# Substitution products in a buffer of their own, low weight parts on VectorE, gate weights a tile ahead: a change to a two-layer hybrid encoder on one core

## The chip, the core and the metric

The kernel runs on one core of a Trainium2 chip. The metric is the device time of one execution in microseconds (us). All data is float32; products that need full precision are made from operands split in a high part (a rounded copy, type fp32r) and a low part (the rest), so that one product costs three matmuls.

The engines are named as the profile names them: PE (matmuls; PEld is its weight load), DVE (VectorE), ACT (ScalarE), POOL (GpSimd) and SP, which here only issues DMAs.

## What is computed

Two layers of an encoder over 1040 positions (16 meta tokens and 1024 inputs) and 1024 channels. Cut to what matters here:

```python
def hybrid_mixer(h, ...):
    proj = h @ w_in                       # q, k, v, z, gates b and a, short-conv channels
    qkv = silu(depthwise_conv(qkv)); q, k = l2norm(q), l2norm(k)
    beta = sigmoid(b_raw); g = -exp(a_log) * softplus(a_raw + dt_bias)
    o = chunk_gated_delta_rule(q, k, v, g[0], beta[0]) \
        + flip(chunk_gated_delta_rule(flip(q), flip(k), flip(v), flip(g[1]), flip(beta[1])))
    o = rms_normalised(o) * dn_norm_w * silu(z)
    y_sc = sc_b * depthwise_conv(sc_c * sc_h)
    return concat(o, y_sc) @ w_out

h = h + hybrid_mixer(rmsnorm(h)); h = h + swiglu(rmsnorm(h))     # twice, then a last rmsnorm
```

The delta rule works in chunks and for each chunk and head it solves a unit triangular system A = I + M, with M = strict triangle of (beta k) k^T times a decay. The kernel uses chunks of 128 and inverts A: forward substitution in the 32 x 32 blocks of the diagonal, and matmuls that join the blocks.

## The kernel before, in words

The activations lie transposed (channels on the partitions, 1040 positions along the row). A dense product (`dense`) takes one tile of 128 output channels in three chunks of 346 to 348 positions, each in a PSUM bank of its own: eight times three matmuls, and then an evacuation on DVE. Three banks carry the name `acc`. The weights of a tile come in two halves of 128 x 512: a DMA into `raw`, the high part on ACT (`wsplit`, L127), the low part on POOL (L128). `lov[0]` would send the low part to DVE; before, it is False throughout.

Order: the program is planned ahead. Each instruction has a priority, which is its place in the program unless it is set otherwise; a planner simulates the run with estimated durations, and each engine then works off its instructions in the fixed order that comes out. `at_prio` sets the running priority. `evp[0]` is a rank far ahead of all others (the layer's base less 60000), used for the evacuations of `dense`; with None they have their place in the program. `mmp[0]` puts dense matmuls of the later tiles behind other PE work. `after(ins, prev)` adds an order between two instructions. A tile with a tag shares a buffer with others of the same tag, and its first writer waits for the last user of the one before.

In each layer:

- Input tiles 4 to 7 (k), then 0 to 3 (q), positions `pos` 0 to 7 of a loop: dense product, evacuation (multiplied by the norm's `rstd`, L283; in the first one or two tiles a copy, L288, because `rstd` is late), convolution (L295 on ACT, L296 and L297 on DVE), silu and square on ACT, sums of squares on PE, `normalise` (L402). The weights of the next tile are loaded at the end of each turn.
- After `pos` 2, `gates()`: weights of 16 gate columns (L316 DMA, L317 high part, L318 low part, in a slot of the `raw` and `whi` rings), a product (L325), small operations. `gt`, in the buffer P0, is its working space.
- At `pos` 4 to 6, `chunk_p`: k k^T of each chunk (L439), the decay with the mask `off` (L443), their product (L448) into P0 and P1, the systems of the two directions.
- `sub_start` copies the diagonal blocks (L501) and transposes them (L503); `substitute(d)`, for directions 0 and 1, runs 31 steps of two DVE operations each: a product of a column of W and a row of Xi (L513), and its subtraction from Xi (L514). All 32 blocks lie along the rows of 128 partitions, so that each works on 128 x (j+1)(31-j) elements. Before, the product is put, transposed, into a part of W that is no longer read; L514 reads it transposed again. The two directions have nothing in common and are interleaved by the planner.
- `invert(d)` transposes the result (L523, L524) and joins the blocks with small matmuls (L543, L549, L555, L567) and copies on ACT.
- Beside these, tiles 8 to 11 (v), each with `v_store` (transposes on PE; L641 copies the first 16 positions, `vm`, on DVE), then z and short-convolution tiles; `chunk_a` makes the attention parts; then the scan over chunks, the output projection and the feed-forward part.

In the program, `substitute(0)` stands ahead of the v tiles, `invert(0)` behind the first of them, `substitute(1)` behind the second and `invert(1)` behind the third.

Of the kernel before, what the change touches and what calls it, by code (L numbers as in the profile page):

```python
# [7 lines left out]
F32 = mybir.dt.float32  # L8
F32R = mybir.dt.float32r
BF16 = mybir.dt.bfloat16  # L10
AF = mybir.ActivationFunctionType
ALU = mybir.AluOpType
# [10 lines left out]
WK = 4  # L23
# [3 lines left out]
C_ID, C_UT, C_LT, C_NF, C_NB, C_SEL, C_SEL2, C_MISC = 0, 128, 256, 384, 512, 640, 656, 672  # L27
# [13 lines left out]
def trunk(ctx: ExitStack, tc: tile.TileContext, xT, w_in, w_ba, w_out, w_gu, w_dn,  # L41
          par_d, alog_d, dtb_d, cst_d, eye_d, out):
    nc = tc.nc
    sb = ctx.enter_context(tc.tile_pool(name="sb", bufs=1))
    wp = ctx.enter_context(tc.tile_pool(name="wp", bufs=3))
# [4 lines left out]
    def nm(p):  # L50
        cnt[0] += 1
        return f"{p}_{cnt[0]}"

    def big(tag, dt=F32):
        return sb.tile([128, 4, L], dt, tag=tag, name=nm(tag))

    def row(tag, dt=F32, bufs=1):
        return sb.tile([128, L], dt, tag=tag, bufs=bufs, name=nm(tag))

    def t2k(tag):  # L60
        return sb.tile([128, 4, 128], F32, tag="ck2", bufs=5, name=nm(tag))

    def c4k(tag="c"):
        return sb.tile([128, L], F32, tag="c", bufs=2, name=nm(tag))
# [4 lines left out]
    def pa():  # L69
        return bank("a")  # L70
# [16 lines left out]
    def after(ins, prev):  # L87

        if prev is not None:
            tc.add_manual_dep(ins.ins, prev.ins.name, dep, reason="order")  # L90
        return ins

    def at_prio(p):
        tc.cur_priority = p
# [3 lines left out]
    tt = nc.vector.tensor_tensor  # L98
# [3 lines left out]
    dma = nc.sync.dma_start  # L102
# [14 lines left out]
    evp = [None]  # L117
    jobs = []
    lov = [False]
# [133 lines left out]
    epsq = sb.tile([128, 1], F32, name="epsq")  # L253
    nc.vector.memset(epsq, HD * EPS)
    cols["eps"] = epsc
    off = sb.tile([128, 2, 128], F32, name="off")
    dma(off.rearrange("p a b -> p (a b)"), cst_d[:, C_NF:C_NF + 256])
    alog = sb.tile([128, 2, 8], F32, name="alog")
    dtb = sb.tile([128, 2, 8], F32, name="dtb")
    dma(alog, alog_d.partition_broadcast(128))  # L260
# [4 lines left out]
    for l in range(DEPTH):  # L265
# [2 lines left out]
        pcol = lambda c: par[:, l * P_L + c:l * P_L + c + 1]  # L268
        rstd = ss
        base = tc.cur_priority  # L270
        evp[0] = base - 60000


        o0 = 16 if last else 0
        ochunks = TAIL if last else FULL
# [1 line left out]
        def inproj(i, evac, pool=None, chunks=FULL):  # L277
            ws = pre.pop(i) if i in pre else wload(w_in[l, i], KT)
            dense(ws, x, chunks, evac, pool)

        def to_row(t):
            def f(ps, n0, n1):
                tt(out=t[:, n0:n1], in0=ps, in1=rstd[:, n0:n1], op=ALU.mult)  # L283
            return f

        def to_row_late(t):
            def f(ps, n0, n1):
                nc.vector.tensor_copy(t[:, n0:n1], ps)  # L288
            return f

        def trow():
            return row(Y[1], F32, 3)

        def conv(src, dst, wc):
            act(out=dst, in_=src, func=AF.Copy, scale=pcol(wc + 1))  # L295
            stt(out=dst[:, 1:L], in0=src[:, 0:L - 1], scalar=pcol(wc), in1=dst[:, 1:L], op0=ALU.mult, op1=ALU.add)  # L296
            stt(out=dst[:, 0:L - 1], in0=src[:, 1:L], scalar=pcol(wc + 2), in1=dst[:, 0:L - 1], op0=ALU.mult, op1=ALU.add)  # L297
# [11 lines left out]
        m0d = dram.tile([2, 2, 4, 16, 16], F32, name=nm("m0d"))  # L309
        rsd = [dram.tile([4, 260], F32, name=nm("rsd")) for _ in range(2)]  # L310


        def gates():
            wr = wp.tile([128, WK, 128], F32, tag="raw", bufs=2, name=nm("war"))[:, 0, :].rearrange("p (k m) -> p k m", k=8)
            wb = wp.tile([128, WK, 128], F32R, tag="whi", name=nm("wba"))[:, 0:2, :].rearrange("p a (b m) -> p (a b) m", m=32)
            dma(wr, w_ba[l])  # L316
            act(out=wb[:, :, 0:16], in_=wr, func=AF.Copy)  # L317
            tt(out=wb[:, :, 16:32], in0=wr, in1=wb[:, :, 0:16].bitcast(F32), op=ALU.subtract)  # L318
            gt = big("P0")
            bat = gt[:, 0, :]  # L320
            for (n0, n1) in FULL:
                ps = pacc()
# [19 lines left out]
            for d in range(2):  # L342
                tt(out=sv[0][:, 36 * d:36 * d + 36].rearrange("p (c h) -> p c h", c=9), in0=psv[:, :, 1, 4 * d:4 * d + 4],
                   in1=dtb[:, l, 4 * d:4 * d + 4].unsqueeze(1).to_broadcast([128, 9, 4]), op=ALU.add)
# [18 lines left out]
            for d in range(2):  # L363
                tt(out=g[:, d], in0=sv[0][:, 36 * d:36 * d + 36].rearrange("p (c h) -> p c h", c=9),
                   in1=nA[:, 4 * d:4 * d + 4].unsqueeze(1).to_broadcast([128, 9, 4]), op=ALU.mult)
# [51 lines left out]
        P0 = [sb.tile([16, 4, 16], F32, tag=f"P0{d}", name=nm("P0")) for d in range(2)]  # L417
# [70 lines left out]

        tmp0 = []
        subs = {}  # L490

        def sub_start():

            tmp0.append(big(Y[0][2]))
            v = [tmp0[0][:, i, 0:1024] for i in range(4)]
            for d in range(2):
                W, Xi = (v[0], v[2]) if d == 0 else [c4k("x")[:, 0:1024] for _ in range(2)]
                W, Xi, dg = (t.rearrange("p (a b) -> p a b", a=32) for t in (W, Xi, v[3 - 2 * d]))
                dma(Xi, eye_d)
                for b in range(4):  # L500
                    act(out=dg[B[b]], in_=Pv[d][B[b], :, B[b]], func=AF.Copy)  # L501

                nc.vector.transpose(out=W, in_=dg.rearrange("p q i -> p i q"))  # L503
                subs[d] = W, Xi

        def substitute(d):
            W, Xi = subs[d]
            for j in (range(0, 31) if d == 0 else range(31, 0, -1)):
                i0, i1, a0, a1 = (j + 1, 32, 0, j + 1) if d == 0 else (0, j, j, 32)
                sh = [128, a1 - a0, i1 - i0]  # L510

                Tm = W[:, a0:a1, i0:i1]
                tt(out=Tm, in0=W[:, i0:i1, j:j + 1].rearrange("p i o -> p o i").to_broadcast(sh), in1=Xi[:, j:j + 1, a0:a1].rearrange("p o a -> p a o").to_broadcast(sh), op=ALU.mult)  # L513
                tt(out=Xi[:, i0:i1, a0:a1], in0=Xi[:, i0:i1, a0:a1], in1=Tm.rearrange("p a i -> p i a"), op=ALU.subtract)  # L514

        def invert(d):
            P_ = Pv[d]
# [70 lines left out]
        seq = (4, 5, 6, 7, 0, 1, 2, 3)  # L588
        for pos, i in enumerate(seq):
            hh = pos % 4  # L590
            t = trow()
            late = pos < (2, 1)[l]
            inproj(i, to_row_late(t) if late else to_row(t), pfirst if l == 0 and pos == 1 else None)
            if late:
                tt(out=t, in0=t, in1=rstd, op=ALU.mult)
            dst = (QT if i < 4 else KTt)[:, hh, :]
            conv(t, dst, P_CV + 3 * i)
            act(out=dst, in_=dst, func=AF.Silu)
            act(out=t, in_=dst, func=AF.Square)
            jobs.append(lambda w="qk"[i >= 4], q=hh, t=t: sums(w, q, t))  # L600
            if pos == 2:
                g, negG, nGb, negE, gl, bkd = gates()
            nxt = seq[pos + 1] if pos < 7 else 8
            if nxt not in pre:
                pre[nxt] = wload(w_in[l, nxt], KT)
            if pos == 4:
                jobs.extend([lambda c=c: k_out(c) for c in range(9)])
            if pos in (4, 5, 6):
                for c in range(3 * pos - 12, 3 * pos - 9):
                    chunk_p(c)  # L610
        sub_start()
        substitute(0)


# [12 lines left out]
        def low(f):  # L627

            here = tc.cur_priority
            at_prio(mmp[0])  # L630
            f()
            mmp[0] = tc.cur_priority
            at_prio(here)

        def v_store(i, v, c0):

            ps = pa()
            if c0 == 0:
                low(lambda: nc.tensor.transpose(ps[0:16, 0:128], v[:, 0:16], ident))
                vm = t2k("vm")[0:16, 0, :]  # L640
                nc.vector.tensor_copy(vm, ps[0:16, 0:128])  # L641
                dma(vkd[0, 0:16, 0, i * 128:(i + 1) * 128], vm)
            else:
                vt = v[:, 16 + 128 * (c0 - 1):16 + 128 * (c0 + 3)]
                for c in range(4):
                    low(lambda: nc.tensor.transpose(ps[:, c * 128:(c + 1) * 128], vt[:, 128 * c:128 * c + 128], ident))
                act(out=vt, in_=ps, func=AF.Copy)
                adma(vkd[c0:c0 + 4, :, 0, i * 128:(i + 1) * 128].rearrange("c p e -> p c e"), vt.rearrange("p (c e) -> p c e", c=4))

        ca = [0, 1, 8, 2, 7, 3, 6, 4, 5]  # L650
        for i in range(4):
            t = trow()
            inproj(8 + i, to_row(t))
            v = trow() if i % 2 == 0 else row(Y[1] + "f")
            conv(t, v, P_CV + 3 * (8 + i))
            act(out=v, in_=v, func=AF.Silu)
            jobs.extend([lambda i=i, v=v, c0=c0: v_store(i, v, c0) for c0 in (0, 1, 5)])
            if i == 0:
                invert(0)
            elif i == 1:  # L660
                substitute(1)
            elif i == 2:
                invert(1)
            if i > 0:
                for c in ca[3 * i - 3:3 * i]:
                    chunk_a(c)
# [164 lines left out]
        for i in range(4):  # L831
            t = trow() if i < 2 else hb[1][:, i, :] if i < 3 else y3
# [95 lines left out]
        for m in range(KT + 2):  # L928
# [4 lines left out]
            k = m - 2  # L933
# [106 lines left out]
        for f in range(FT):  # L1040
# [6 lines left out]
            W = {}  # L1047
# [8 lines left out]
            end = f == FT - 1  # L1056
# [105 lines left out]
        for gi, grp in enumerate(GROUPS):  # L1162
# [19 lines left out]
            if gi == 0:  # L1182

                w2 = {}
                for m in range(0, KT, 2):
                    hi, lo = (wp.tile([128, WK, 128], F32R, tag=t, name=nm(t)) for t in ("whi", "wlo"))
                    raw = raw4(("raw", "ck2")[m // 2 % 2])
# [104 lines left out]
```

## Time and profile before

| | us |
|---|---|
| median of 3 runs (2689.06 to 2693.82) | 2690.77 |
| the profiled execution, its own time | 2690.32 |
| its span, first to last instruction | 2688.5 |
| granted clock over the span | 0.98 |

Times in the profile count from the start of the span. A page gives the busy time of each engine; views of it give the same for stretches of time, list who waited for whom (in total, how often, the longest), or list single instructions: start, duration, engine, line, operation, output and inputs, shapes, and in brackets the idle time of the engine before it with what ended it. The clock is the share of full speed at which PE was allowed to run.

### The profile page before, as it was taken

The page shows a single profiled execution, that of the slowest core. Times are in us where ns is not written, and L with a number is a line of the kernel's source. Part 1 is how long each engine was busy: PE and PEld are TensorE (multiplying, and loading weights), DVE is VectorE, ACT ScalarE, POOL GpSimd, SP SyncE. Part 2 cuts the span into 40 slices and gives each one's busy share as a digit, 9 for nine tenths or more (in the row PEclk, how much of TensorE's full clock was granted, in tenths as well). Part 3 has the DMA queues.
Part 4 walks back from the last instruction along what each step waited for, and adds up shares of the span by engine and source line. Part 5 has one row for each costly group of instructions (what it writes and reads, how often), then busy time and mean ns, then how long its engine had stood idle before and what let it go on. Part 6 is the DMA issues. An engine that isn't in the chain of part 4 may idle for free. (4 is left out here: it accounts for less than half of the span.)

```text
span 2688.5 us, 43950 instructions
## 1 busy us (share of the span) xinstructions
PE 2564.2 (95%) x17274; PEld 2348.5 (87%) x17274; DVE 1533.5 (57%) x2245; ACT 985.8 (37%) x1785; POOL 1129.2 (42%) x823
## 2 busy tenths in 40 slices
PE   7988999999999999999999889999999999999997
PEld 6988889988999999999998878899877888887886
DVE  6787333548766566622355874345587766644226
ACT  4663322435333333321245633134452333332224
POOL 3353121225666666543222322212267766663341
PEclk9999899999999999999999989999999999999998
DMA  3532585434312222532224425766342222225321
GB/s 106 153 123 87 167 263 184 158 119 142 108 60 72 86 77 76 189 112 69 75 89 144 139 79 170 254 197 211 98 132 94 63 82 75 91 88 182 93 81 63
DMA packets 181492, 326.13 MB, mean 121 GB/s; under 512 B 21681, under 2 KB 58805, under 8 KB 181285
## 3 DMA queue, kind: packets, MB, share of 16 engines
q1 hardware_dynamic: 147972, 272.64, 31.0%
q10 hardware_dynamic: 30496, 42.09, 5.2%
q0 software_dynamic: 2816, 8.59, 1.0%
q8 instruction: 136, 2.23, 0.3%
q14 instruction: 72, 0.58, 0.1%
HBM read 239.66 MB, written 83.58 MB: 120 GB/s over the span
## 5 line engine op out<-in xcount | busy, mean ns | idle before, releaser
L128 POOL TENSOR_TENSOR wlo<-raw,whi 128x512 fp32r<-128x512 f32 (+2 forms) x264 | 337.7, 1282 | 1015.4 <-ACT whi L127 852.7
L154 PE MATMUL pacc<-a,whi 128*128 128x346 f32 (+2 forms) x1031 | 349.5, 342 | 13.3 <-ACT whi L127 6.4
L156 PE MATMUL pacc<-a,wlo 128*128 128x346 f32 (+2 forms) x1031 | 347.7, 340 | 4.1 <-POOL wlo L128 4.1
L127 ACT ACTIVATE whi<-raw 128x512 fp32r<-128x512 f32 (+2 forms) x264 | 151.3, 577 | 509.6 <-PE pacc L155 286.7
L154 PE MATMUL pacc<-b,whi 128*128 128x346 f32 (+2 forms) x882 | 307.1, 349 | 9.9 <-DVE a L283 9.4
L155 PE MATMUL pacc<-a,whi 128*128 128x346 f32 (+2 forms) x916 | 312.4, 342 | 2.7 <-DVE a L838 2.6
L156 PE MATMUL pacc<-b,wlo 128*128 128x346 f32 (+2 forms) x882 | 305.6, 349 | 0.3 <-POOL wlo L128 0.3
L155 PE MATMUL pacc<-b,whi 128*128 128x346 f32 (+2 forms) x776 | 267.8, 346 | 0.0
L154 PEld LDWEIGHTS pacc<-a,whi 128*128 128x128 f32 x1031 | 198.7, 193 | 25.5 <-ACT whi L127 7.4
L156 PEld LDWEIGHTS pacc<-a,wlo 128*128 128x128 f32 x1031 | 198.6, 193 | 11.6 <-POOL wlo L128 4.7
L154 PEld LDWEIGHTS pacc<-b,whi 128*128 128x128 f32 x882 | 168.8, 192 | 23.8 <-DVE a L283 10.8
L155 PEld LDWEIGHTS pacc<-a,whi 128*128 128x128 f32 x916 | 176.8, 193 | 10.2 <-DVE a L838 2.8
L156 PEld LDWEIGHTS pacc<-b,wlo 128*128 128x128 f32 x882 | 168.9, 192 | 11.4 <-issue 1.0
L981 POOL TENSOR_TENSOR wlo<-rw,whi 128x512 fp32r<-128x512 f32 x92 | 134.8, 1467 | 72.5 <-ACT whi L980 66.9
L155 PEld LDWEIGHTS pacc<-b,whi 128*128 128x128 f32 x776 | 148.6, 192 | 8.5 <-issue 0.4
L981 POOL TENSOR_TENSOR a<-rw,a 128x512 fp32r<-128x512 f32 x64 | 107.0, 1675 | 66.9 <-ACT a L980 66.9
L981 POOL TENSOR_TENSOR b<-rw,b 128x512 fp32r<-128x512 f32 x64 | 90.2, 1412 | 85.1 <-ACT b L980 53.4
L843 DVE TENSOR_TENSOR a<-pacc,a 128x346 f32<-128x346 f32 (+2 forms) x116 | 57.8, 500 | 109.4 <-PE pacc L156 109.2
L980 ACT ACTIVATE whi<-rw 128x512 fp32r<-128x512 f32 x92 | 57.8, 631 | 140.3 <-DVE rw L1054 72.8
L843 DVE TENSOR_TENSOR b<-pacc,b 128x512 f32<-128x512 f32 (+1 forms) x88 | 52.5, 599 | 98.9 <-PE pacc L156 98.1
L1055 DVE TENSOR_TENSOR rw<-raw,rw 128x512 f32<-128x512 f32 x44 | 97.2, 2208 | 1.2
L1050 DVE TENSOR_TENSOR rw<-rw,rw 128x512 f32<-128x512 f32 x44 | 66.9, 1521 | 48.1 <-POOL wlo L981 31.4
(813 smaller groups left out, 7365.7 us busy)
## 6 DMA issues: line engine op xcount, KB each, us to landing
raw<-in_w_in SPq DMA_DIRECT2D x112, 256.0 KB, 2.6
raw<-in_w_gu SPq DMA_DIRECT2D x104, 256.0 KB, 2.9
rw<-in_w_gu SPq DMA_DIRECT2D x88, 256.0 KB, 2.8
rec<-aqd SPq DMA_DIRECT2D x62, 256.0 KB, 4.1
rec<-vkd SPq DMA_DIRECT2D x61, 256.0 KB, 3.7
raw<-in_w_dn SPq DMA_DIRECT2D x60, 256.0 KB, 2.8
raw<-in_w_out SPq DMA_DIRECT2D x48, 256.0 KB, 3.0
a<-ad SPq DMA_DIRECT2D x20, 520.0 KB, 3.9
```

The source lines that it names most:

```text
L127: act(out=hi, in_=raw[:, 0:kk, :], func=AF.Copy)
L128: (tt if lov[0] else ptt)(out=lo, in0=raw[:, 0:kk, :], in1=hi.bitcast(F32), op=ALU.subtract)
L154: mm(ps[:, :n], wh, xh[:, n0:n1], start=(k == 0), stop=False)
L155: mm(ps[:, :n], wh, xl[:, n0:n1], start=False, stop=False)
L156: mm(ps[:, :n], wl, xh[:, n0:n1], start=False, stop=(k == K - 1))
L843: tt(out=hr[m][:, n0:n1], in0=ps, in1=hr[m][:, n0:n1], op=ALU.add)
L980: act(out=hi, in_=src, func=AF.Copy)
L981: ptt(out=lo, in0=src, in1=hi.bitcast(F32), op=ALU.subtract)
L1050: tt(out=s1t, in0=A21, in1=A22, op=ALU.add)
L1055: tt(out=A21, in0=A11, in1=A21, op=ALU.subtract)
```

## The change

- The mask `off` is loaded in each layer, into a buffer of 1 KB a partition with the tag `off`. When the layer is done with it, that buffer becomes `Tm`, for the products of the substitution.
- The product is laid out as rows of Xi are (i, then a), densely packed in `Tm`. Its operands are a column of W, broadcast along the inner dimension, and a row of Xi, broadcast along the outer one; the subtraction reads three operands with an inner step of one element.
- Direction 1's first product is ordered behind direction 0's last subtraction.
- `lov[0]` is True from `pos` 4 until `substitute(1)` has been put down, so the low parts of tiles 1, 2, 3, 8 and 9 of each layer go to DVE.
- The gate weights are loaded and split at the start of `pos` 2, ahead of that tile's product, into free parts of P0 and P1.
- The evacuations get their rank from `pos` 2 on, not from the start of the layer.
- The copy L641 gets the rank of the evacuations.

```diff
--- before.py
+++ after.py
@@ -253,8 +253,6 @@
     epsq = sb.tile([128, 1], F32, name="epsq")
     nc.vector.memset(epsq, HD * EPS)
     cols["eps"] = epsc
-    off = sb.tile([128, 2, 128], F32, name="off")
-    dma(off.rearrange("p a b -> p (a b)"), cst_d[:, C_NF:C_NF + 256])
     alog = sb.tile([128, 2, 8], F32, name="alog")
     dtb = sb.tile([128, 2, 8], F32, name="dtb")
     dma(alog, alog_d.partition_broadcast(128))
@@ -268,8 +266,6 @@
         pcol = lambda c: par[:, l * P_L + c:l * P_L + c + 1]
         rstd = ss
         base = tc.cur_priority
-        evp[0] = base - 60000
-
 
         o0 = 16 if last else 0
         ochunks = TAIL if last else FULL
@@ -309,14 +305,20 @@
         m0d = dram.tile([2, 2, 4, 16, 16], F32, name=nm("m0d"))
         rsd = [dram.tile([4, 260], F32, name=nm("rsd")) for _ in range(2)]
 
-
-        def gates():
-            wr = wp.tile([128, WK, 128], F32, tag="raw", bufs=2, name=nm("war"))[:, 0, :].rearrange("p (k m) -> p k m", k=8)
-            wb = wp.tile([128, WK, 128], F32R, tag="whi", name=nm("wba"))[:, 0:2, :].rearrange("p a (b m) -> p (a b) m", m=32)
+        off = sb.tile([128, 2, 128], F32, tag="off", name=nm("off"))
+        dma(off.rearrange("p a b -> p (a b)"), cst_d[:, C_NF:C_NF + 256])
+
+
+        gt = big("P0")
+        wr = gt[:, 3, 0:128].rearrange("p (k m) -> p k m", k=8)
+        wb = big("P1", F32R)[:, 0, 0:256].rearrange("p (k m) -> p k m", k=8)
+
+        def gate_weights():
             dma(wr, w_ba[l])
             act(out=wb[:, :, 0:16], in_=wr, func=AF.Copy)
             tt(out=wb[:, :, 16:32], in0=wr, in1=wb[:, :, 0:16].bitcast(F32), op=ALU.subtract)
-            gt = big("P0")
+
+        def gates():
             bat = gt[:, 0, :]
             for (n0, n1) in FULL:
                 ps = pacc()
@@ -488,10 +490,13 @@
 
         tmp0 = []
         subs = {}
+        Tm = None
 
         def sub_start():
 
+            nonlocal Tm
             tmp0.append(big(Y[0][2]))
+            Tm = sb.tile([128, 2, 128], F32, tag="off", name=nm("Tm")).rearrange("p a b -> p (a b)")
             v = [tmp0[0][:, i, 0:1024] for i in range(4)]
             for d in range(2):
                 W, Xi = (v[0], v[2]) if d == 0 else [c4k("x")[:, 0:1024] for _ in range(2)]
@@ -505,13 +510,14 @@
 
         def substitute(d):
             W, Xi = subs[d]
+            prev = subs.get("end")
             for j in (range(0, 31) if d == 0 else range(31, 0, -1)):
                 i0, i1, a0, a1 = (j + 1, 32, 0, j + 1) if d == 0 else (0, j, j, 32)
-                sh = [128, a1 - a0, i1 - i0]
-
-                Tm = W[:, a0:a1, i0:i1]
-                tt(out=Tm, in0=W[:, i0:i1, j:j + 1].rearrange("p i o -> p o i").to_broadcast(sh), in1=Xi[:, j:j + 1, a0:a1].rearrange("p o a -> p a o").to_broadcast(sh), op=ALU.mult)
-                tt(out=Xi[:, i0:i1, a0:a1], in0=Xi[:, i0:i1, a0:a1], in1=Tm.rearrange("p a i -> p i a"), op=ALU.subtract)
+                sh = [128, i1 - i0, a1 - a0]
+                t = Tm[:, 0:sh[1] * sh[2]].rearrange("p (a b) -> p a b", a=sh[1])
+                after(tt(out=t, in0=W[:, i0:i1, j:j + 1].to_broadcast(sh), in1=Xi[:, j:j + 1, a0:a1].to_broadcast(sh), op=ALU.mult), prev)
+                prev = None
+                subs["end"] = tt(out=Xi[:, i0:i1, a0:a1], in0=Xi[:, i0:i1, a0:a1], in1=t, op=ALU.subtract)
 
         def invert(d):
             P_ = Pv[d]
@@ -588,6 +594,10 @@
         seq = (4, 5, 6, 7, 0, 1, 2, 3)
         for pos, i in enumerate(seq):
             hh = pos % 4
+            if pos == 2:
+                gate_weights()
+                evp[0] = base - 60000
+            lov[0] = pos > 3
             t = trow()
             late = pos < (2, 1)[l]
             inproj(i, to_row_late(t) if late else to_row(t), pfirst if l == 0 and pos == 1 else None)
@@ -638,7 +648,11 @@
             if c0 == 0:
                 low(lambda: nc.tensor.transpose(ps[0:16, 0:128], v[:, 0:16], ident))
                 vm = t2k("vm")[0:16, 0, :]
+                here = tc.cur_priority
+                at_prio(evp[0])
                 nc.vector.tensor_copy(vm, ps[0:16, 0:128])
+                evp[0] = tc.cur_priority
+                at_prio(here)
                 dma(vkd[0, 0:16, 0, i * 128:(i + 1) * 128], vm)
             else:
                 vt = v[:, 16 + 128 * (c0 - 1):16 + 128 * (c0 + 3)]
@@ -659,6 +673,7 @@
                 invert(0)
             elif i == 1:
                 substitute(1)
+                lov[0] = False
             elif i == 2:
                 invert(1)
             if i > 0:
```

## Prediction

> **What bounds the kernel now.** I read the head of the page first, then the busy time by stage, then who waits for whom on PE, then single instructions in order of time.
>
> ```profile
> span 2688.5 us, 43950 instructions
> ...
> PE 2564.2 (95%) x17274; PEld 2348.5 (87%) x17274; DVE 1533.5 (57%) x2245; ACT 985.8 (37%) x1785; POOL 1129.2 (42%) x823
> ```
>
> PE is busy for 2564 of 2688 us, so a change that leaves its matmuls alone, as this one does, can only win part of the other 124 us, and what a throttled clock costs. The busy time by stage (columns PE, PEld, DVE, ACT, POOL, then the granted clock) shows where the diff's stages stand in this:
>
> ```profile
> 100.00:160.00 60.00, 55.71 (x371) 52.02 (x370) 42.31 (x55) 45.13 (x94) 32.95 (x71) 0.97 0.71 223
> 160.00:245.00 85.00, 69.67 (x448) 65.94 (x447) 82.30 (x158) 34.08 (x41) 27.84 (x15) 0.90 0.21 67
> ...
> 1440.00:1500.00 60.00, 55.56 (x382) 51.65 (x375) 43.54 (x56) 44.98 (x97) 28.63 (x46) 1.00 0.70 227
> 1500.00:1590.00 90.00, 73.18 (x448) 64.91 (x447) 85.34 (x158) 37.09 (x44) 21.80 (x15) 0.92 0.24 73
> ```
>
> 160 to 245 and 1500 to 1590 are the substitution stages of the two layers. DVE is full there (82.3 of 85, 85.3 of 90), and PE idles 15.3 and 16.8 us, 32.1 in all. The clock costs more: 0.10 of 85 and 0.08 of 90 us is 15.7 us of missing clock. In the stages just before, DVE has 17.7 and 16.5 us free.
>
> PE's waits, in total, times and longest, from 100 to 260, from 1500 to 1700, and from 0 to 100:
>
> ```profile
> PE pacc L154 <- DVE b L283: 5.1, 2, 3.5
> PE pf L543 <- DVE b L523: 4.6, 1, 4.6
> PE pacc L156 <- POOL wlo L128: 3.6, 1, 3.6
> ```
> ```profile
> PE pacc L154 <- DVE a L283: 9.4, 3, 5.9
> ...
> PE pa L646 <- DVE vm L641: 3.5, 1, 3.5
> ...
> PE pf L543 <- DVE a L523: 1.6, 1, 1.6
> ```
> ```profile
> PE pacc L325 <- DVE wba L318: 3.5, 1, 3.5
> ```
>
> L283 empties the accumulators, L523 opens the inversion behind the substitution, L641 is the small copy of v, L318 the low part of the gate weights. Nearly everything that PE waits for here is DVE, late in a queue whose order was fixed beforehand.
>
> **The change part by part: gate weights.**
>
> ```profile
> 44.16 6.67 DVE L194 RECIPROCAL rstd<-rstd 128x348 f32<-128x348 f32 x3 [4.39 <-ACT rstd L193]
> 50.76 1.30 DVE L283 TENSOR_TENSOR b<-pacc,rstd 128x348 f32<-128x348 f32 x3
> ...
> 53.47 4.00 PE L325 MATMUL pacc<-a,wba 128*32 128x348 f32 x15 [3.51 <-DVE wba L318]
> ```
>
> PE reaches the gates 3.5 us before the low part is there. Split a tile ahead, that wait goes; next late is the accumulator, which the first of the three L283 frees at about 51.2 us. So 53.47 - 51.2 = **2.3 us** (bounds 0 and 3.5). In layer 1 PE has no such wait: nothing. P0 and P1, which now take these weights, were read last by the previous layer's down projection, over before the gates; the weight loads behind this DMA on SP would wait with it if the planner set it too early, which I cost at nothing.
>
> **Evacuations of the first two tiles** lose their rank until the third.
>
> ```profile
> 32.61 2.31 DVE L184 TENSOR_TENSOR rstd<-rstd,sq 128x1040 f32<-128x1040 f32 x1 [0.40 <-POOL rstd L184]
> ```
>
> In layer 0 this addition to the norm, earlier in the program, may now come first, 2.3 us; three accumulators cover one late copy, so nothing (at worst +2.3; at best the norm ends sooner by a copy or two). The **reload of the mask** is one more 128 KB DMA in layer 1, far ahead of its use: nothing.
>
> **The copy of v** gets the evacuations' rank, so it waits for one running operation, not a stretch of the queue. Of the 3.5 us I take **3.0** (bounds 0 and 3.5).
>
> **Low parts.** In layer 0, POOL's L128 by stretch of time, and its mean on the page:
>
> ```profile
> 0.00:62.00 62.00, 9.61 (x6) 0.94 0.34 111
> 62.00:100.00 38.00, 8.37 (x7) 1.00 0.24 71
> 100.00:160.00 60.00, 9.03 (x7) 0.97 0.71 223
> ```
> ```profile
> L128 POOL TENSOR_TENSOR wlo<-raw,whi 128x512 fp32r<-128x512 f32 (+2 forms) x264 | 337.7, 1282 | 1015.4 <-ACT whi L127 852.7
> ```
>
> Two per tile: 20 by 160 us are ten tiles, the eight of the normalised rows and two of v. The moved five a layer are the last of these ten, so they leave before the substitution, and PE's 3.6 us for POOL at 217 us stays. Twenty operations leave POOL (20 x 1.28 = 26 us) for DVE, where 128x512 takes 0.69 us (row L807 below): 13.8 us in both layers, beside 34 us that DVE idles there. Nothing, then; up to +13.8 if each fell in front of an evacuation; below nothing, as collisions with POOL go.
>
> **Substitution.** First the price of a step. The start of d=0 alone, then both directions interleaved, then the tail of d=1 between other work:
>
> ```profile
> 165.21 0.37 DVE L513 TENSOR_TENSOR b<-b 128x112 f32<-128x112 f32 x1
> 165.61 0.37 DVE L514 TENSOR_TENSOR b<-b 128x112 f32<-128x112 f32 x1
> 166.02 0.40 DVE L513 TENSOR_TENSOR b<-b 128x135 f32<-128x135 f32 x1
> ```
> ```profile
> 213.67 0.56 DVE L513 TENSOR_TENSOR x<-x,x 128x256 f32<-128x256 f32 x1
> 214.16 0.53 DVE L514 TENSOR_TENSOR b<-b 128x231 f32<-128x231 f32 x1
> ...
> 241.83 0.20 DVE L514 TENSOR_TENSOR x<-x,x 128x112 f32<-128x112 f32 x1
> ```
>
> Alone, each operation starts 0.03 to 0.04 us after the one it needs has ended. Interleaved, the next starts before the last has ended (0.49 us between starts, 0.56 long): some 0.07 to 0.09 us overlap. One direction at a time gives that overlap up, about 0.12 us on each of 124 operations, 15 us a layer.
>
> Against it stands the layout. For contiguous operands, and one broadcast along the inner dimension:
>
> ```profile
> L402 DVE TENSOR_TENSOR b<-b,bc x8: 1228/1242/1754, 110.0 to 274.5; 128x1040 f32<-128x1040 f32 x8
> ```
> ```profile
> L807 DVE TENSOR_TENSOR a3f<-a3f,st x8: 678/692/1907, 1835.6 to 1908.3; 128x512 f32<-128x512 f32 x8
> ```
>
> 1.242 and 0.692 us give 0.161 us and 1.04 ns an element, so 256 elements 0.427 us against 0.56 and 112 elements 0.277 against 0.37. I put the excess down to the operand that steps 32 elements (a column of W in L513, the transposed product in L514), which the change makes contiguous or broadcast. The 0.20 us row speaks against that; it had other work in front of it. The Trainium skill, SBUF — State Buffer, section "Door 1: The DMA port swizzle", says that an access pays whenever it crosses into another 16-byte line; by that rule all of this excess goes, and the rows that have it agree but for the one named.
>
> A direction multiplies and subtracts sums of (j+1)(31-j), 5456 elements each: 10,912 in 62 operations, both directions 21,824 in 124. After: 124 x 0.161 + 21,824 x 0.00104 = 42.7, gaps 124 x 0.035 = 4.3: 47 us of DVE a layer. Before, the two lines by stretch in layer 0 (L513, then L514):
>
> ```profile
> 160.00:200.00 40.00, 12.78 (x27) 0.91 0.22 68
> 200.00:245.00 45.00, 16.46 (x36) 0.89 0.20 66
> ```
> ```profile
> 160.00:200.00 40.00, 12.20 (x25) 0.91 0.22 68
> 200.00:245.00 45.00, 19.27 (x37) 0.89 0.20 66
> ```
>
> 60.7 us, less 124 overlaps of 0.09 counted twice (11): about 50. So DVE gains only some 3 us a layer: its time hardly changes, its order does. If the excess stays, it is 124 x 0.12 us worse.
>
> ```profile
> 237.58 1.91 PE L543 MATMUL pf<-b,P 32*32 32x32 f32 x64 [4.63 <-DVE b L523]
> ```
>
> Direction 0 now comes first: 23.5 us of its own chain, in a stage where (82.3 - 50) / 85 of DVE goes to other work, is 23.5 / 0.62 = 38 us from its start a little before 165. So the inversion that PE awaits here until 237.6 can start some 35 us earlier, beside direction 1; evacuations contend with one chain instead of two. The wait that the change adds (direction 1's first product behind direction 0's last) is on DVE itself and in its order, so nothing queues behind it that would not anyway. The products' buffer waits for the mask's last reader, before the stage.
>
> Waits for L283 and L523 were 5.1 + 9.4 + 4.6 + 1.6 = 20.7 us, some of it outside the stage, and much of it lateness that a fixed order will produce again. I take two fifths, **8.3** (bounds: none of it, and all 20.7 with POOL's 3.6). With the copy of v that removes 11.3 of 32.1 idle us, 35%; the same share of the missing clock is **5.5** (bounds 0 and 15.7).
>
> Sum: 2.3 + 3.0 + 8.3 + 5.5 = 19.1. The profiled execution took 2690.3 us (span 2688.5), 0.5 below the median of the runs: 2690.3 - 19.1 = **2671**.
>
> **Rivals.** *All of it goes*: 3.5 + 3.5 + 20.7 + 3.6 + 15.7 = 47.0, so 2643; more likely about 2652. For it: DVE's real order would come close to the planned one. Against: waits for ACT and POOL beside these stay. The Trainium skill, VectorE: DVE Perf Modes, section "The DRAIN you can't avoid", measured eight chained copies equally long with a semaphore after each as with one; by that rule serialising is free and this rival gains. The 0.49 and 0.40 us steps above differ from it.
>
> *The gaps only move*: the new order makes waits of the same size elsewhere, and the gates' and copy's 5.3 us are lost to them: 2690, within 2685 to 2696. For it: PE's order is fixed beforehand and every gap here has another cause close behind (POOL's 3.6 us, the accumulators).
>
> *The serial chain is slower*: if contiguous products keep the excess, the DVE stage grows by 15 - 3 = 12 to 15 us in each layer, where DVE has none free. Half of 30 reaching PE, with 3 of clock and less 5.3 for gates and copy, is +13: **2703**; all of it 2718. It decides from where a 256-element product takes longer than about 0.46 us (0.49 less the gap). For it: the 0.20 us row. Against: L807's row.
>
> **How the numbers follow.** Forecast (2660 to 2684) 0.56, all of it goes 0.14, gaps only move 0.14, slower 0.16. About 0.2%, 5.4 us, is what a measurement of this kernel can tell from no change; so faster 0.70, same 0.14, slower 0.16. 2650 to 2703 leaves out half of the slower case and a third of the first rival.
>
> **What would show it.** Right: a 256-element L513 or L514 near 0.43 us; L523 of direction 0 near 200 us instead of 235.6, with PE's small products beside direction 1; waits for wba and vm gone from PE's list; the clock of 160 to 245 above 0.93. Wrong: L513 still 0.56 us; DVE full for longer than 85 us; PE waiting for L283 in 0 to 60 us (lost rank) or 100 to 160 (low parts in front).

## The result, and the profile after

| | us |
|---|---|
| before, median of 4 runs (2689.06 to 2693.82) | 2690.81 |
| changed, median of 4 runs (2665.95 to 2674.99) | 2670.83 |
| ratio, 95% interval | 0.9924 [0.9904, 0.9944] |
| profiled execution of the changed kernel, its span | 2667.5 |

The change makes the kernel 0.76% faster, 20 us, where 2671 was forecast. The experiments show that the number was met partly by luck: some terms of the sum came to nothing, and a loss that was not in it cancels a gain that was put too low.

The head of the page of the changed kernel:

```profile
span 2667.5 us, 43943 instructions
...
PE 2559.5 (96%) x17274; PEld 2343.7 (88%) x17274; DVE 1528.0 (57%) x2265; ACT 988.5 (37%) x1785; POOL 1088.5 (41%) x803
```

PE's work is the same; its idle time fell from 124 to 108 us. Where, the busy time by stage of the changed kernel tells (PE, PEld, DVE, ACT, POOL, granted clock):

```profile
100.00:160.00 60.00, 52.57 (x350) 48.39 (x350) 42.43 (x59) 39.46 (x80) 25.90 (x68) 0.97 0.64 203
160.00:245.00 85.00, 79.99 (x786) 75.52 (x786) 77.12 (x150) 45.43 (x57) 19.34 (x17) 0.98 0.24 77
245.00:320.00 75.00, 67.80 (x779) 63.74 (x778) 35.81 (x53) 25.97 (x38) 16.65 (x13) 0.83 0.54 177
...
1500.00:1590.00 90.00, 86.98 (x833) 77.88 (x831) 76.87 (x151) 43.84 (x58) 25.05 (x21) 1.00 0.26 84
1590.00:1680.00 90.00, 80.13 (x779) 68.45 (x779) 36.33 (x47) 24.17 (x37) 17.77 (x15) 0.87 0.59 185
```

In the two substitution stages PE's idle time fell from 15.3 to 5.0 and from 16.8 to 3.0 us, and the clock rose from 0.90 to 0.98 and from 0.92 to 1.00. Part of it is given back right behind them. Of the kernel before, the stretches that follow were:

```profile
245.00:320.00 75.00, 70.86 (x1035) 66.31 (x1035) 31.80 (x42) 31.49 (x47) 16.58 (x14) 0.93 0.54 171
...
1590.00:1680.00 90.00, 85.77 (x1068) 74.69 (x1067) 35.62 (x43) 34.52 (x51) 23.59 (x18) 0.94 0.50 162
```

There PE's idle time rose from 4.1 to 7.2 and from 4.2 to 9.9 us, and the clock fell from 0.93 to 0.83 and from 0.94 to 0.87.

Over the four stretches, PE's idle time falls from 40.5 to 25.1 us. The missing clock, estimated as in the prediction (the share that is missing, times the length of the stretch), does not fall: it is 26.4 us before and 26.2 us after. What leaves the two stages comes back right behind them.

The products of the inversion by line (min, median and longest in ns, then first and last start), first of the kernel before, then of the changed one; `pf` is direction 0, `pb` direction 1:

```profile
L543 PE MATMUL pf<-b,P x128: 191/224/254, 237.6 to 255.9; 32*32 32x32 f32 x128
...
L543 PE MATMUL pb<-b,P x128: 191/191/212, 290.5 to 303.9; 32*32 32x32 f32 x128
```
```profile
L549 PE MATMUL pf<-b,P x128: 191/191/212, 214.2 to 229.7; 32*32 32x32 f32 x128
...
L549 PE MATMUL pb<-b,P x128: 184/224/258, 284.4 to 298.9; 32*32 32x32 f32 x128
```

The first inversion starts 23 us earlier, the second only 6: 70 us now lie between their starts instead of 53. The substitution stage itself does not get shorter. Its first product and its last subtraction in layer 0, before and then changed:

```profile
163.21 0.21 DVE L513 TENSOR_TENSOR b<-b 128x31 f32<-128x31 f32 x1
...
244.68 0.20 DVE L514 TENSOR_TENSOR x<-x,x 128x31 f32<-128x31 f32 x1
```
```profile
166.46 0.21 DVE L518 TENSOR_TENSOR Tm<-b 128x31 f32<-128x31 f32 x1
...
248.56 0.19 DVE L520 TENSOR_TENSOR x<-x,Tm 128x31 f32<-128x31 f32 x1
```

That is 81.7 us from start to end before and 82.3 us after; in layer 1 it is 80.2 and 83.0. The chain, in the changed kernel:

```profile
232.31 0.42 DVE L518 TENSOR_TENSOR Tm<-x,x 128x256 f32<-128x256 f32 x1
232.77 0.43 DVE L520 TENSOR_TENSOR x<-x,Tm 128x256 f32<-128x256 f32 x1
233.23 0.42 DVE L518 TENSOR_TENSOR Tm<-x,x 128x255 f32<-128x255 f32 x1
```

256 elements take 0.42 us, as forecast (0.427), and the next begins 0.03 to 0.04 us after the end, a step of 0.46 us. The two lines in layer 0, L518 and then L520, by busy time:

```profile
200.00:250.00 50.00, 15.48 (x41) 0.97 0.23 77
...
sum 90.00, DVE 24.02; mean DVE 12.01
```
```profile
200.00:250.00 50.00, 18.69 (x41) 0.97 0.23 77
...
sum 90.00, DVE 30.31; mean DVE 15.15
```

Together 54.3 us, where before it was 60.7. This sum still counts twice what overlaps between the two lines. Counted once, from the same rows, DVE spends 57.5 us on them before and 54.3 after (59.0 and 52.7 in layer 1). Some operations take far longer than the rest:

```profile
243.26 1.15 DVE L520 TENSOR_TENSOR x<-x,Tm 128x175 f32<-128x175 f32 x1
```

In layer 0, twelve of the 124 operations of the changed kernel take 1.1 to 2.4 us, 16.6 us together; before, eight take over 0.9 us, 10.7 us together.

### The profile page after: what moved, and what is told of

It is laid out like the page before. It is cut to its first block, busy times and chain, and to the rows that moved or that the text cites. A ratio compares the mean times of both kernels' runs of the same rounds, so it can differ in the third digit from the quotient of the medians.

```text
span 2667.5 us, 43943 instructions
## 1 busy us (share of the span) xinstructions
PE 2559.5 (96%) x17274; PEld 2343.7 (88%) x17274; DVE 1528.0 (57%) x2265; ACT 988.5 (37%) x1785; POOL 1088.5 (41%) x803
## 5 line engine op out<-in xcount | busy, mean ns | idle before, releaser
L128 POOL TENSOR_TENSOR wlo<-raw,whi 128x512 fp32r<-128x512 f32 x244 | 294.6, 1210 | 941.2 <-ACT whi L127 857.5
L154 PE MATMUL pacc<-a,whi 128*128 128x346 f32 (+2 forms) x1031 | 347.3, 340 | 10.6 <-ACT whi L127 7.5
L154 PE MATMUL pacc<-b,whi 128*128 128x346 f32 (+2 forms) x882 | 303.3, 345 | 1.7 <-ACT whi L127 1.1
L155 PE MATMUL pacc<-b,whi 128*128 128x346 f32 (+2 forms) x776 | 265.8, 343 | 1.1 <-DVE b L853 1.1
L996 POOL TENSOR_TENSOR wlo<-raw,whi 128x512 fp32r<-128x512 f32 x50 | 77.5, 1552 | 34.5 <-ACT whi L995 25.9
```

The source lines that it names most:

```text
L128: (tt if lov[0] else ptt)(out=lo, in0=raw[:, 0:kk, :], in1=hi.bitcast(F32), op=ALU.subtract)
L154: mm(ps[:, :n], wh, xh[:, n0:n1], start=(k == 0), stop=False)
L155: mm(ps[:, :n], wh, xl[:, n0:n1], start=False, stop=False)
L996: ptt(out=lo, in0=src, in1=hi.bitcast(F32), op=ALU.subtract)
```

## The experiments

Twelve kernels, in three groups; each ratio stands against the kernel before on the same chip, whose median was 2685.4, 2686.8 and 2690.4 us in the three. Theory A is that of the prediction: the substitution edit gains in its stage, most of all by its order, and gate weights and copy add 5 us. The rivals are that the gain comes from the other edits (B), and that DVE's time in the substitution is what counts, so that the order costs.

**The substitution edit alone (s_both).** `sub_start` and `substitute` as in the change's diff, and the mask, without its other edits.

> The kernel before with the substitution edit alone: products in the 1 KB buffer, densely packed, direction 1 behind direction 0, mask loaded per layer. Theory A (the substitution edit frees PE in its own stage, and that is most of the gain): 2676 to 2680, 10 to 15 us faster. Theory B (what its stage wins, the second inversion, now alone and at a low clock, gives back; the gain comes from the other edits): 2687 to 2692.

2667.0 us, ratio 0.9930 [0.9912, 0.9948]: 14 to 24 us faster, at the upper end of theory A's 10 to 15 or above it. All of the gain is here.

**The rest alone (r_rest).** The change's diff without `sub_start` and `substitute`.

> All edits except the substitution: gate weights early, rank of evacuations from the third tile, low parts of ten tiles on DVE, rank of the copy of v, mask loaded per layer; products stay in W, directions interleaved. Theory A: 2682 to 2686 (gates and copy 5 to 8 us, the others nothing). Theory B: 2672 to 2678, nearly the whole gain.

2686.8 us, 1.0002 [0.9989, 1.0014]. Nothing: neither theory A's 5 to 8 us nor theory B's gain. B falls.

**The dense layout without the order (s_layout).**

```diff
+            Tms.append(tmp0[0][:, 3, 0:256])
+            Tms.append(sb.tile([128, 2, 128], F32, tag="off", name=nm("Tm")).rearrange("p a b -> p (a b)"))
...
-                Tm = W[:, a0:a1, i0:i1]
...
+                t = Tms[d][:, 0:sh[1] * sh[2]].rearrange("p (a b) -> p a b", a=sh[1])
+                tt(out=t, in0=W[:, i0:i1, j:j + 1].to_broadcast(sh), in1=Xi[:, j:j + 1, a0:a1].to_broadcast(sh), op=ALU.mult)
+                tt(out=Xi[:, i0:i1, a0:a1], in0=Xi[:, i0:i1, a0:a1], in1=t, op=ALU.subtract)
```

> The kernel before with the dense layout alone: direction 0's products in a free quarter of its working tile, direction 1's in the 1 KB buffer, no order between the directions, so the planner can interleave them. If the speed of DVE is what counts (256 elements at 0.42 us and the overlap of 0.08 us kept, 15 us less DVE a layer): 2672 to 2680, no worse than both edits. If the order is what counts: 2684 to 2691.

2654.9 us, 0.9883 [0.9865, 0.9902]: 31 us faster, 12 us more than with the order and more than either expectation (at most 19). Its chain, both directions interleaved:

```profile
202.64 0.41 DVE L516 TENSOR_TENSOR Tm<-x,x 128x256 f32<-128x256 f32 x1
202.98 0.39 DVE L517 TENSOR_TENSOR b<-b 128x231 f32<-128x231 f32 x1
203.29 0.41 DVE L517 TENSOR_TENSOR x<-x,Tm 128x256 f32<-128x256 f32 x1
```

0.41 us long, but 0.31 to 0.34 us between starts, against 0.46 in the changed kernel and 0.49 before. The stage and the one behind it:

```profile
160.00:245.00 85.00, 81.11 (x777) 76.25 (x776) 71.42 (x162) 44.18 (x55) 24.39 (x20) 0.99 0.28 94
245.00:320.00 75.00, 71.29 (x842) 67.48 (x842) 29.21 (x42) 23.27 (x37) 13.53 (x10) 0.87 0.51 166
...
1500.00:1590.00 90.00, 82.49 (x806) 73.58 (x805) 67.45 (x140) 34.70 (x47) 29.44 (x23) 1.00 0.31 104
1590.00:1680.00 90.00, 87.09 (x849) 76.02 (x849) 37.18 (x50) 26.37 (x41) 20.58 (x14) 0.96 0.58 195
```

DVE is full for 71 and 67 us instead of 82 and 85, and the stretch behind keeps PE busier (3.7 and 2.9 us idle) than the changed kernel's.

**The order without the dense layout (s_order).**

```diff
+            prev = subs.get("end")
...
-                tt(out=Tm, in0=W[:, i0:i1, j:j + 1].rearrange("p i o -> p o i").to_broadcast(sh), ...)
-                tt(out=Xi[:, i0:i1, a0:a1], ...)
+                after(tt(out=Tm, in0=W[:, i0:i1, j:j + 1].rearrange("p i o -> p o i").to_broadcast(sh), ...), prev)
+                prev = None
+                subs["end"] = tt(out=Xi[:, i0:i1, a0:a1], ...)
```

> The kernel before with the order alone: direction 1 behind direction 0, products still transposed in W. If the order is what counts (first inversion earlier): 2678 to 2686. If DVE's speed counts, a serial chain without the dense layout costs 12 to 15 us of DVE a layer: 2695 to 2715, the slower rival of the prediction.

2698.6 us, 1.0038 [1.0024, 1.0052]: slower, by 6 to 14 us. A product takes longer and each waits for the last:

```profile
191.14 0.63 DVE L514 TENSOR_TENSOR b<-b 128x256 f32<-128x256 f32 x1
191.81 0.63 DVE L516 TENSOR_TENSOR b<-b 128x256 f32<-128x256 f32 x1
192.47 0.62 DVE L514 TENSOR_TENSOR b<-b 128x255 f32<-128x255 f32 x1
```

Steps of 0.66 us against 0.49. Yet its first inversion starts earlier than that of the layout run (the rows are of s_order, then of s_layout):

```profile
L545 PE MATMUL pf<-b,P x128: 191/191/236, 219.3 to 234.9; 32*32 32x32 f32 x128
...
L545 PE MATMUL pb<-b,P x128: 184/224/258, 295.0 to 309.8; 32*32 32x32 f32 x128
```
```profile
L546 PE MATMUL pf<-b,P x128: 191/191/212, 221.1 to 237.0; 32*32 32x32 f32 x128
...
L546 PE MATMUL pb<-b,P x128: 191/191/212, 273.3 to 286.3; 32*32 32x32 f32 x128
```

An earlier first inversion alone does not make the kernel faster: here the second comes later. What it is worth at an equal length of the stage is taken up below the table.

**Gate weights alone (g_gates).**

```diff
-            wr = wp.tile([128, WK, 128], F32, tag="raw", ...)
-            wb = wp.tile([128, WK, 128], F32R, tag="whi", ...)
+        wr = gt[:, 3, 0:128].rearrange("p (k m) -> p k m", k=8)
+        wb = big("P1", F32R)[:, 0, 0:256].rearrange("p (k m) -> p k m", k=8)
...
+            if pos == 2:
+                gate_weights()
```

> The kernel before with the gate weights a tile ahead, alone. Theory A: the wait of 3.5 us for the low part goes, the gates' product starts 3.5 us earlier and runs at full clock (5 us by its end in the changed kernel): 2685 to 2688. Theory B says the same of this part. If the fixed order makes up for it later: 2690 to 2692.

2689.8 us, 1.0016 [1.0004, 1.0028]: not faster, slightly slower. The gain at the gates is there and is lost again:

```profile
49.05 1.14 PE L328 MATMUL pacc<-a,P 128*32 128x348 f32 x6 [0.85 <-DVE b L283]
```
```profile
236.98 1.22 PE L546 MATMUL pf<-b,P 32*32 32x32 f32 x38 [3.81 <-DVE b L526]
```

PE is at the gates 4.4 us earlier than before (53.47) and at the first inversion 0.6 us earlier (237.58). The lead is not lost in waiting for the inversion's transpose, which takes 3.8 us now and took 4.6 before. It is gone before the substitution begins, whose first product starts at 164.6 us (before, at 163.2). Between 100 and 165 us, PE's products k k^T now wait for the products of `chunk_p` on DVE, a wait that the kernel before does not have there:

```profile
PE pb L442 <- DVE P L451: 5.1, 3, 2.8
```

Why the whole is 1 to 8 us slower stays open.

**Low parts alone (l_low).**

```diff
+            lov[0] = pos > 3
...
                 substitute(1)
+                lov[0] = False
```

> The kernel before with the low parts of tiles 1, 2, 3, 8 and 9 of each layer on DVE, alone. Prediction: nothing, 2688 to 2693 (DVE idles beside them). If 13.8 us of DVE fall in front of evacuations: 2694 to 2704. If freeing POOL's queue for the normalisation counts: 2680 to 2687.

2685.7 us, 0.9996 [0.9984, 1.0009]: nothing, as forecast. In the changed kernel the twenty take 0.68 us each on DVE, from 80 us on.

**Rank of the copy of v alone (v_vm).**

```diff
+                at_prio(evp[0])
                 nc.vector.tensor_copy(vm, ps[0:16, 0:128])
+                evp[0] = tc.cur_priority
+                at_prio(here)
```

> The kernel before with the rank of the copy of v alone. Prediction: 3 us faster, 2686 to 2689, PE's wait for vm gone. If the gap only moves: 2690 to 2692.

2686.4 us, 0.9995 [0.9982, 1.0009]: no gain that shows, though the interval (5 us faster to 2 us slower) does not exclude the 3 us. PE's waits for it between 1500 and 1700 fell from 3.5 to 1.0 us, the wait for the evacuations there rose from 9.4 to 11.6:

```profile
PE pacc L154 <- DVE a L283: 11.6, 4, 5.9
...
PE pa L650 <- DVE vm L643: 1.0, 1, 1.0
```

**The mask alone (p_mask).** `off` is loaded in each layer, into the buffer with the tag `off`.

> The kernel before with the mask loaded in each layer and nothing else, one more 128 KB DMA far ahead of its use: a measure of how much the plan alone moves the time. If the plan is stable: 2690 to 2692. If any small edit shifts the plan by some us: off by more than 4 us to either side, and the parts can't be added up.

2687.1 us, 1.0005 [0.9993, 1.0017], 2 us faster to 5 us slower. By this one edit, the plan is stable enough for effects of 10 us and more to be compared; effects of a few us can't be told from it.

**The changed kernel without its order (x_inter).** `sub_start` and `substitute` of s_layout in place of the change's, all other edits kept.

> The changed kernel with its order taken out: direction 0's products in a free quarter of its working tile, direction 1's in the 1 KB buffer, directions interleaved; all other edits kept. If the order costs what the overlap of 0.12 us on 124 operations a layer is worth and the other edits are worth nothing: 2652 to 2659, as the dense layout alone. If the order helped together with the other edits: 2667 to 2675, as the changed kernel.

2655.8 us, 0.9866 [0.9846, 0.9885]: 36 us faster than before, not to be told from the layout alone (0.9883 [0.9865, 0.9902]). Both beat the changed kernel.

**The order on top of the layout run (s_lay_ord).** The `after` and `prev` lines of s_order added to s_layout, with its two buffers.

> The dense layout alone, in the same two buffers as in the layout run, and the order between the directions. If the order is what costs: 2664 to 2670, 10 to 15 us above the layout run, as with both edits in one buffer. If it was the shared buffer or the reload of the mask: 2653 to 2658.

2677.2 us, 0.9940 [0.9921, 0.9959]. Against 0.9883 that is about 15 us for the order alone, and with one buffer (s_both, 0.9930) it is much the same; the buffers have no part that shows.

**Products in their own buffers, but transposed (t_pack).**

```diff
-                sh = [128, i1 - i0, a1 - a0]
+                sh = [128, a1 - a0, i1 - i0]
...
-                tt(out=t, in0=W[:, i0:i1, j:j + 1].to_broadcast(sh), in1=Xi[:, j:j + 1, a0:a1].to_broadcast(sh), op=ALU.mult)
+                tt(out=t, in0=W[:, i0:i1, j:j + 1].rearrange("p i o -> p o i").to_broadcast(sh), ...)
-                tt(out=Xi[:, i0:i1, a0:a1], in0=Xi[:, i0:i1, a0:a1], in1=t, op=ALU.subtract)
+                tt(out=Xi[:, i0:i1, a0:a1], in0=Xi[:, i0:i1, a0:a1], in1=t.rearrange("p a i -> p i a"), op=ALU.subtract)
```

> The layout run with the products in the same buffers of their own, but transposed as before, now packed: the product steps 32 elements in W's column along the inner dimension, the subtraction reads the product with a step of 1 to 31. If the strided operands cost the time: 2680 to 2690 and 0.5 us or more for 256 elements. If it was the place in W: 2653 to 2660 and 0.42 us.

2689.9 us, 1.0001 [0.9985, 1.0016]. The buffer as such is worth nothing.

```profile
212.65 0.56 DVE L516 TENSOR_TENSOR Tm<-x,x 128x256 f32<-128x256 f32 x1
213.14 0.54 DVE L517 TENSOR_TENSOR b<-b 128x231 f32<-128x231 f32 x1
213.61 0.57 DVE L517 TENSOR_TENSOR x<-x,Tm 128x256 f32<-128x256 f32 x1
```

**Only the product's loop turned (t_half).**

```diff
-                tt(out=t, in0=W[:, i0:i1, j:j + 1].to_broadcast(sh), ...)
+                sh = [128, n_a, n_i]
+                tt(out=t.rearrange("p i a -> p a i"), in0=W[:, i0:i1, j:j + 1].rearrange("p i o -> p o i").to_broadcast(sh), ...)
```

> The layout run with the product's loop turned alone: it reads W's column with a step of 32 along the inner dimension and writes the dense buffer in steps; the subtraction stays dense. If each strided operand costs its own operation: product at 0.5 us or more for 256 elements, subtraction at 0.42; time half way, 2666 to 2676.

2679.7 us, 0.9960 [0.9944, 0.9976], between the two, nearer to before than expected. The strided product is slow, the dense subtraction fast:

```profile
207.12 0.62 DVE L518 TENSOR_TENSOR Tm<-x,x 128x256 f32<-128x256 f32 x1
207.67 0.38 DVE L519 TENSOR_TENSOR b<-b 128x231 f32<-128x231 f32 x1
207.97 0.40 DVE L519 TENSOR_TENSOR x<-x,Tm 128x256 f32<-128x256 f32 x1
```

Over the kernels, from the DVE rows of each profiled execution, both layers together: the time that DVE spends on the two lines (overlaps counted once), and the length of the two stages, each from the first product to the last subtraction. The last column is the measured change against the kernel before.

| kernel | order | DVE on the two lines, us | stages, us | time, us |
|---|---|---|---|---|
| before | no | 116.5 | 161.9 | 0 |
| t_pack | no | 118.4 | 163.7 | 0 |
| t_half | no | 103.2 | 148.4 | -11 |
| s_layout | no | 86.0 | 132.6 | -31 |
| x_inter | no | 84.1 | 130.7 | -36 |
| s_order | yes | 139.4 | 192.6 | +10 |
| s_lay_ord | yes | 108.9 | 163.0 | -16 |
| s_both | yes | 109.7 | 162.2 | -19 |
| changed | yes | 107.0 | 165.3 | -20 |

Among the five kernels without the order, the time follows the length of the stages about one for one: 13.5 us shorter gave 11, 29 gave 31, 31 gave 36. The four with the order lie below that line. In three of them the stages are as long as before, and they are 16 to 20 us faster; in s_order they are 31 us longer, and the kernel is 10 us slower. So the order does two things. It makes the stages about 30 us longer (132.6 to 163.0, 161.9 to 192.6), and for stages of one length it goes with some 17 to 23 us less time. The earlier first inversion, which now runs beside direction 1, can account for this, but no run isolates it.

What the order costs beyond the stages is seen in x_inter, the changed kernel without it:

```profile
245.00:320.00 75.00, 67.34 (x909) 63.08 (x907) 29.57 (x41) 23.23 (x37) 14.54 (x10) 0.91 0.52 163
...
1590.00:1680.00 90.00, 86.22 (x870) 75.05 (x869) 32.40 (x47) 26.79 (x41) 19.70 (x14) 0.98 0.56 184
```

In these two stretches behind the stages it misses 8.6 us of clock, by the same estimate, and the changed kernel 24.5. Over all four stretches the changed kernel has 3.8 us more idle time of PE and 12.4 us more missing clock, together 16.2, and its span is 16.2 us longer (2667.5 against 2651.3). Between s_layout and s_lay_ord it is 10.6 us of idle time and 13.6 of clock, where the spans differ by 27.9.

## Why the prediction was right or wrong, point by point

- **What bounds the kernel**: right in the main. The gain came out of PE's idle time (124 to 108 us), and it was won in the substitution stages. "Nearly everything" was too strong: DVE ended 27 of the 40 us of waits that the lists for 100 to 260 and 1500 to 1700 give.
- **Gate weights 2.3 us and copy of v 3.0 us**: these two terms failed. All the small edits together measure 1.0002 [0.9989, 1.0014], at most 3 us faster. At the gates PE even gained 4.4 us, above the bound of 3.5, and lost it again within 110 us. That the gaps only move was a rival for the whole change; it held for this part.
- **Low parts, mask**: nothing, as forecast. PE's 3.6 us for POOL, which were said to stay, are 2.3 us in l_low and gone in the changed kernel. The evacuations' rank was not run alone; within the rest it is part of nothing.
- **Price of a dense operation**: right, 0.427 forecast, 0.42 measured, and the cause is the strided operand, shown by t_half and t_pack. The SBUF rule of the Trainium skill (SBUF — State Buffer, section "Door 1: The DMA port swizzle") agrees with these rows of 256 elements; the single row of 0.20 us that spoke against it stays unexplained. The total was too low: 42.7 us of operations were forecast for a layer and 54.3 measured in layer 0, because the long operations, 16.6 us there, were not in it.
- **Price of the order**: right in kind, an overlap lost on 124 operations a layer. Dense, the step goes from 0.31 to 0.34 us to 0.46. s_order is the slower rival as it was described, without its deciding condition: forecast +13 with 5.3 us of other gains in it (so +18 alone), measured +10.
- **"So DVE gains only some 3 us a layer: its time hardly changes, its order does."** This held for the changed kernel: 3.2 us in layer 0 and 6.3 in layer 1, with stages as long as before. It is partly luck, because both sides were too low, 57.5 us measured for "about 50" and 54.3 for 42.7 without the gaps. What the sentence hides is that its two sides can be had apart: the layout is worth 31 us alone and 29 on top of the order (1.0038 to 0.9930), while the order costs 10 us alone and 12 to 15 on top of the layout.
- **The first inversion "some 35 us earlier"**: it started 23 us earlier in layer 0 and 37 in layer 1, where the stage itself began 11 us earlier.
- **Two fifths of DVE's waits, 8.3, and 35% of the clock, 5.5**: mis-sized, and this is where the mechanism fell short. Within the two stages PE's idle time fell by 24.1 us, where 11.3 were forecast with the copy of v, and the missing clock by 14.0, where 5.5 were. Behind the stages the prediction put nothing ("nothing queues behind it that would not anyway"); there 8.7 us of idle time and 13.8 us of missing clock came back. The net in these four stretches is 15.6 us against 16.8 forecast, and the substitution edit alone measured 18.8 (14 to 24) against 13.8. With 5.3 that did not come, the sum met 2671: a gain put too low, a loss left out and two terms that came to nothing.
- **All of it goes, about 2652**: not this change, but its layout without its order, 2655.

What stays open: why the clock is low (0.83 and 0.87) where the second inversion stands further behind the first, and whether the earlier first inversion is all that the order is worth for stages of one length. Both go with the order in every run.

## What to carry to other kernels

Price a serial chain on a busy engine by the step between starts, with and without independent work between its links: 0.31 to 0.46 us here for operations of the same length. Two effects of one edit that cancel on paper are two experiments; one of them was worth keeping alone. When an edit moves work out of a full stage, price the stretch that it moves to as well: here most of the clock won in the stage was missing behind it. And a wait that is removed is a gain only if no other wait behind it takes its place.

## What the runs showed of the hardware that had not been expected

For 128x256 float32 on DVE, an operand read with a step of 32 elements, or of 16 (the subtraction of t_pack), makes 0.56 to 0.63 us of 0.41 to 0.43. In t_pack that step falls from 31 to 1, and the excess is full at a step of 4, small at 3 and gone at 2. With a step of 4, and then of 2:

```profile
230.29 0.35 DVE L517 TENSOR_TENSOR b<-b 128x112 f32<-128x112 f32 x1
...
232.68 0.22 DVE L517 TENSOR_TENSOR b<-b 128x60 f32<-128x60 f32 x1
```

Dense, these sizes take 0.27 and 0.22 us (changed kernel); with a step of 32, at the same place in the kernel before, 0.35 and 0.25.

Interleaved with an independent chain, dense operations of 0.41 us start every 0.31 to 0.34 us; dependent ones every 0.46. Eight copies with a semaphore after each took as long as with one by the Trainium skill (VectorE: DVE Perf Modes, section "The DRAIN you can't avoid"). No run here repeats those copies. In this chain, where each operation needs the one before, the trace does not agree that serialising is free: 0.12 to 0.15 us a step are lost against the interleaved form.
